# A two-layer decoder step on one core: the first layer's planned order is made anew

## The chip, the cores and the metric

The kernel runs on one core of one Trainium2 chip. The metric is the device time of one execution of the whole program, in microseconds (us); the median of several runs counts. In the names of the profile PE is the matrix engine (its matmuls; PEld its weight loads), DVE, ACT and POOL are the three engines for elementwise work, and SP is the engine that issues most transfers. A matmul's weights are its stationary operand.

## The reference

One step of a decoder with two layers, for a prompt of 512 tokens and 8 sequences of 8 new tokens (576 tokens in all, width 1024). The first layer is a gated DeltaNet, the second a differential attention over shared K and V with 64 pages of cache. Everything is float32. Only the first layer is touched by the change:

```python
shift, scale, gate = ada_split(c, ada_w_a, ada_b_a, 3)
h = modulate(x, norm_a, shift, scale)              # RMS norm, gain, shift
proj = h @ w_in                                    # q, k, v, z, beta, a
q, k, v = split(silu(causal_conv(conv_buf, qkv, conv_w)))   # width 4
a = tril(kb @ k.T * decay, -1)                     # per chunk of the tokens
t_inv = triangular_solve(eye + a, eye)             # an inverse per chunk and head
u, w = t_inv @ (v * beta), t_inv @ (kb * exp(g))
# along the chunks: v_new = u - w @ s;  o = (q * exp(g)) @ s + qk @ v_new
#                   s = s * exp(g_last) + (k * exp(g_last - g)).T @ v_new
y = (rms_norm(o, out_gain) * silu(z)) @ w_out
x = x + gate * y
```

The outputs are the tokens' results of both layers, the states of the DeltaNet and of the convolution (for the prompt and for each of the 8 sequences), and K and V.

## The kernel before

**Numbers.** Weights come in chunks of 128 x 1024. Each projection of a chunk is made in fp32r with a weight split in two parts, hi (the rounded weight, `whi`) and lo (the rest, `wlo`), and an activation split alike (`hhi`, `hlo`): 24 products of 128x288 for each half of the tokens (hlo with hi and hhi with hi for 8 slices, then hhi with lo for 8 slices). The other products are in plain fp32.

**First stretch.** `body` loads x, makes the norm, and goes in eight steps k over the eight slices of the features: a pair of products for shift and scale (`ada_pair`), then the slice's `modulate` (POOL and ACT). Three weights are loaded at k = WAT = 3, and their products are made slice by slice (`part`, recorded at L241). Then `phase_a` begins.

**The woven first layer.** The work on 16 heads, in 8 groups of two, is written as some dozens of generators: the conv of each tile (`conv`), the decays, `prep` (norms, k k and q k products, result `ckq`), the inverse of the chunks (`tinv_pe`, on 32x16 and 32x32 blocks), the `chain` over four chunks with its outputs, the samples' part (`tinv_s`, `sample_gdn`, `sample_states`), and `post` with its two heads. A generator yields the engine that it needs next, a cost in us and its conditions. `Weave.drive` steps that generator which the planner thinks can start first; of those that can start at once, that with the lowest rank. What is emitted so is pinned: on PE, ACT, DVE and POOL the order of the program is the order of the plan, and an engine waits at an instruction whose data isn't there. The plan's costs are numbers in the source; a transfer counts as landed a fixed time after its issue (7.0 for a weight).

**Weights in the woven part.** The weight sets j are in three rooms in turn (two of `whi`/`wlo`, one of two `wraw` tiles). `first_parts` issues hi (a transfer that casts, POOL's queue, L711), `negatives` writes its negative into lo on ACT (L719), `second_parts` adds the weight onto it by an accumulating transfer (POOL's queue, L727). `weave_proj` (L731) emits the products of a chunk in pieces of 4 products. The projections run in the order of `TILES`, then 8 chunks of the output projection (`out_half`) over the first eight heads. All woven products are recorded at L431, transposes at L435.

**Behind it.** `out_a` (the second half of the output projection) and the second layer are written out in order, with weights over `loadw`: a raw weight into `wraw` (SP's queue, L214), a cast on ACT (L217) and a difference on POOL (L218).

Of the kernel before, what the change touches and what calls it, by code (L numbers as in the profile page):

```python
# [26 lines left out]
G = 8  # L27
# [68 lines left out]
TILES = [(i + (t in "kq"), t) for i in range(G) for t in "vwkqzy" if i + (t in "kq") < G]  # L96
# [148 lines left out]
def ada_loads(K, W, A):  # L245
    at = 0.0
    for n, kt in enumerate(K.kts):
        yield None, 0, at, Room("araw")
        at = W.now + ADA
        ch = A.araw.tile([128, 8, 128], F32, name="araw")  # L250
        W.araw = ch, W.took[0]
        K.nc.sync.dma_start(out=ch[:], in_=K.ada[kt].rearrange("p (k m) -> p k m", m=128))
        W.done[("araw", n)] = W.now + 7.0, None
# [148 lines left out]
ENGINE = {"E": "E", "A": "A", "D": "D", "S": "D", "P": "P", "Q": "P"}  # L402


class Weave:
# [4 lines left out]

    def __init__(self, K):
        self.K, self.n, self.now = K, 0, 0.0
        self.free = dict.fromkeys("EADP", 0.0)
        self.port = 0.0
        self.done, self.live = {}, []
# [5 lines left out]
    def matmul(self, **kw):  # L421
# [6 lines left out]
        else:  # L428
            cost = 0.3 if n == 128 else 0.134 if n == 64 else 0.03 if n == 32 else 0.02
        self.cost += cost  # L430
        return self.K.nc.tensor.matmul(**kw)  # L431

    def transpose(self, **kw):
        self.cost += 0.11
        return self.K.nc.tensor.transpose(**kw)  # L435

# [3 lines left out]
    def leave(self, *rooms):  # L440

        self.later += [(self.left, r) for r in rooms]

# [18 lines left out]
    def ready(self, w):  # L462
# [3 lines left out]
        for c in [w[4]] + conds:  # L466
# [10 lines left out]
            x = max(x, t if e is None else t + ((0.0 if eng == "E" else 0.06) if eng and e and ENGINE[e] == ENGINE[eng] else PAD if eng == "E" else HOP))  # L477
        return x

    def drive(self):  # L480
        while self.live:
            x, w = math.inf, None
            for v in self.live:
# [8 lines left out]
            self.now, self.cost, self.later, self.rank, self.took = x, cost or 0.0, [], w[0], []  # L492
# [6 lines left out]
            w[4] = end  # L499
            if eng:  # L500
# [19 lines left out]
def gates(K, A, W, pss):  # L520
# [36 lines left out]
    W.done[("gcd",)] = W.now + 6.0, None  # L557
# [52 lines left out]
def phase_a(K, A, ctx, first):  # L610
# [14 lines left out]
    for name, bufs, roomy in (("u", UB, 1), ("y", YB, 1), ("v", 1, 1), ("z", 4, 1), ("ss", 1, 1), ("araw", 1, 1), ("cso", 2, 1),  # L625
                              ("kq", 2, 0), ("kt", 2, 0), ("vr", 4, 0), ("ck", 2, 0), ("adsb", 1, 0), ("ln", 1, 0),
# [7 lines left out]
    for name in ("pp", "pp", "pc", "po", "pa", "ps"):  # L634
        W.taken[name] += 1
    A.XC = A.ln.tile([128, 2, 8, 16], F32, name="XC")
# [7 lines left out]
    W.add(1, gates(K, A, W, first[0]))  # L644
    W.sets = {}
    W.add(4, first_parts(K, W, n + 1))
    W.add(4, negatives(K, W, n + 1))
    W.add(4, second_parts(K, W, n + 1))
# [3 lines left out]
    for s in groups:  # L652
        for rank, work in ((1, s.decays()), (1, s.prep()), (0, s.inverse()), (0, s.chunks()), (3, s.sample()), (2, s.post())):
# [10 lines left out]
HOP = 0.2  # L664
CONV = 6
PAD = 0.4
ADA = 11.5
UB = 2
YB = 1
# [31 lines left out]
def first_parts(K, W, n):  # L701


    for j, src in enumerate(sources(K, n)):
        yield "Q", 0.7, Room(f"set{j % 3}")
        if j % 3 < 2:
            hi, lo = (p.tile([128, 8, 128], F32R, name=n) for p, n in ((K.whi, "whi"), (K.wlo, "wlo")))
        else:
            hi, lo = (K.wraw.tile([128, 8, 128], F32, name="wraw")[:].bitcast(F32R) for _ in range(2))
        W.sets[j] = hi, lo, W.took[0]  # L710
        K.nc.gpsimd.dma_start(out=hi[:], in_=src)  # L711
        W.done[("hi", j)] = W.now + 7.0, None


def negatives(K, W, n):
    for j in range(n):
        yield "A", 1.05, ("hi", j)
        hi, lo, _ = W.sets[j]
        K.nc.scalar.activation(out=lo[:], in_=hi[:].bitcast(F32), func=AF.Copy, scale=-1.0)  # L719
# [3 lines left out]
def second_parts(K, W, n):  # L723

    for j, src in enumerate(sources(K, n)):
        yield "Q", 0.9, ("neg", j)
        K.nc.gpsimd.dma_start(out=W.sets[j][1][:], in_=src, accum_op=ALU.add)  # L727
        W.done[("w", j)] = W.now + 8.0, None


def weave_proj(K, W, j, evac, heads=None, slots=None):  # L731


    for half in range(2):
        yield "E", None, ("hi", j), Room("pp"), *([("h", heads), ("h", heads + 1)] if heads is not None else [])
        room, = W.took
# [1644 lines left out]
```

## Time and profile before

| | |
|---|---|
| runs | 1369.69, 1358.03, 1357.48 us, median 1358.03 |
| profiled execution | 1357.92 us, its span 1355.9 us |
| PE matmuls busy | 1252.6 us (92%), 13045 matmuls |
| DVE, ACT, POOL busy | 803.4, 719.5, 443.0 us |
| mean granted clock of PE | 0.955 of full speed |
| first stretch | 0 to about 62 us of the span |
| woven first layer | about 62 to 755 us |
| end of the first layer, second layer | from about 755 us |

PE busy is the time in which a matmul was under way, at whatever clock was granted. A clock of 0.50 means that the same work takes twice as long and still counts as busy. So both the idle time of PE and the stretches with a clock under 1.00 are to be looked at, and where they lie.

### The profile page before, as it was taken

How to read it: one execution, taken by the hardware profiler on the slowest of the kernel's cores; microseconds unless marked ns; L12 is line 12 of the kernel's file. 1: busy time of each engine (PE TensorE's matmuls, PEld its weight loads, DVE VectorE, ACT ScalarE, POOL GpSimd, SP SyncE). 2: the span in 40 equal slices, each digit the busy share in tenths (PEclk: the TensorE clock that was granted, in tenths of full speed). 3: DMA queues.
4: the chain of work that ended last, by engine and by line, in shares of the span. 5: the costliest groups of instructions: out<-in, count | busy, mean ns of one | idle time of the engine just before them, and what ended most of it. 6: DMA issues, size and time to landing. Idle time of an engine off the chain costs nothing. (4 is left out here: it accounts for less than half of the span.)

```text
span 1355.9 us, 33987 instructions
## 1 busy us (share of the span) xinstructions
PE 1252.6 (92%) x13045; PEld 1085.9 (80%) x13045; DVE 803.4 (59%) x2263; ACT 719.5 (53%) x1981; POOL 443.0 (33%) x812
## 2 busy tenths in 40 slices
PE   7889999999999898999889699699999999989988
PEld 4679898988878797897778598699888778757888
DVE  5467574766847575485652558688752455555461
ACT  3465767657675575765625332254443465555440
POOL 3423322222222122222111252945562343424232
PEclk7979999999999798999899799799999999999999
DMA  9186676584847466488475355121787877886333
GB/s 362 49 226 179 155 202 150 165 209 125 240 99 202 113 166 163 124 198 239 137 207 154 120 163 187 32 77 51 256 287 227 270 222 248 277 267 203 112 119 114
DMA packets 86643, 240.59 MB, mean 177 GB/s; under 512 B 14338, under 2 KB 26498, under 8 KB 86482
## 3 DMA queue, kind: packets, MB, share of 16 engines
q1 hardware_dynamic: 70642, 180.75, 40.5%
q0 software_dynamic: 15840, 57.68, 19.4%
q8 instruction: 103, 1.69, 0.5%
q14 instruction: 58, 0.48, 0.1%
HBM read 212.55 MB, written 25.84 MB: 176 GB/s over the span
## 5 line engine op out<-in xcount | busy, mean ns | idle before, releaser
L241 PE MATMUL pp<-hhi,whi 128*128 128x288 f32 x640 | 195.6, 309 | 18.8 <-ACT hhi L371 11.0
L241 PE MATMUL pp<-hlo,whi 128*128 128x288 f32 x640 | 194.1, 304 | 1.3 <-DVE hlo L1275 0.6
L241 PE MATMUL pp<-hhi,wlo 128*128 128x288 f32 x640 | 191.9, 301 | 0.0
L431 PE MATMUL pp<-hlo,whi 128*128 128x288 f32 x576 | 173.8, 322 | 2.0 <-DMA whi<-wall 1.7
L431 PE MATMUL pp<-hhi,whi 128*128 128x288 f32 x576 | 162.0, 301 | 0.0
L218 POOL TENSOR_TENSOR wlo<-wraw,whi 128x1024 fp32r<-128x1024 f32 x50 | 119.8, 2397 | 117.7 <-ACT whi L217 110.1
L241 PEld LDWEIGHTS pp<-hhi,whi 128*128 128x128 f32 x640 | 121.2, 191 | 28.0 <-ACT hhi L371 11.7
L241 PEld LDWEIGHTS pp<-hlo,whi 128*128 128x128 f32 x640 | 122.0, 191 | 7.5 <-issue 2.3
L431 PE MATMUL pp<-hhi,wraw 128*128 128x288 f32 x576 | 127.9, 307 | 0.0
L241 PEld LDWEIGHTS pp<-hhi,wlo 128*128 128x128 f32 x640 | 121.9, 191 | 2.1 <-issue 1.7
L431 PEld LDWEIGHTS pp<-hlo,whi 128*128 128x128 f32 x576 | 112.3, 195 | 8.1 <-issue 3.3
L431 PEld LDWEIGHTS pp<-hhi,whi 128*128 128x128 f32 x576 | 112.3, 195 | 0.2
L431 PE MATMUL pp<-hhi,wlo 128*128 128x288 f32 x576 | 102.5, 309 | 0.0
L217 ACT CAST whi<-wraw 128x1024 fp32r<-128x1024 f32 x50 | 52.3, 1048 | 89.7 <-PE pp L241 53.6
L431 PEld LDWEIGHTS pp<-hhi,wraw 128*128 128x128 f32 x576 | 97.8, 196 | 1.5 <-issue 0.8
L879 DVE SCALAR_TENSOR_TENSOR y<-u,vec,y 128x600 f32<-128x600 f32 x96 | 81.8, 853 | 18.2 <-ACT y L876 17.5
L431 PE MATMUL pp<-hlo,wraw 128*128 128x288 f32 x288 | 87.0, 321 | 0.0
L431 PEld LDWEIGHTS pp<-hhi,wlo 128*128 128x128 f32 x576 | 83.7, 193 | 2.6 <-issue 1.3
L727 POOL DMA_DIRECT2D wlo<-wall x37 | 32.9, 890 | 134.5 <-ACT wlo L719 66.9
L1535 POOL TENSOR_TENSOR wm<-w,con_mask 96x512 fp32r<-96x512 f32 x32 | 35.1, 1098 | 95.2 <-PE ps L431 90.5
L1940 DVE TENSOR_REDUCE mx<-sc 128x1 f32<-128x128 f32 (+3 forms) x64 | 31.4, 490 | 58.4 <-PE sc L1922 58.3
L1767 POOL COPY pg<-ptt 1x1 int32<-1x1 int32 x128 | 29.2, 237 | 100.7 <-PE pS L1797 40.3
(487 smaller groups left out, 3183.5 us busy)
## 6 DMA issues: line engine op xcount, KB each, us to landing
pg<-ck SPq DMA_DIRECT2D x64, 512.0 KB, 4.8
pg<-cv SPq DMA_DIRECT2D x64, 512.0 KB, 4.7
wraw<-wall SPq DMA_DIRECT2D x50, 512.0 KB, 4.1
araw<-ada SPq DMA_DIRECT2D x48, 512.0 KB, 4.7
whi<-wall POOLq DMA_DIRECT2D x37, 512.0 KB, 5.7
wlo<-wall POOLq DMA_DIRECT2D x37, 512.0 KB, 5.9
wraw<-wall POOLq DMA_DIRECT2D x36, 512.0 KB, 6.1
araw<-ada SPq DMA_DIRECT2D x8, 1024.0 KB, 13.8
```

The lines of the kernel that those rows point to most:

```text
L217: nc.scalar.copy(out=hi[:], in_=raw[:])
L218: nc.gpsimd.tensor_sub(out=lo[:], in0=raw[:], in1=hi[:].bitcast(F32))
L241: K.mm(out=ps[:, :HT], lhsT=w[a][:, k, :], rhs=h[b][:, k, half * HT:half * HT + HT], start=(k == 0 and a + b == 0), stop=(k == 7 and a == 1))
L431: return self.K.nc.tensor.matmul(**kw)
L727: K.nc.gpsimd.dma_start(out=W.sets[j][1][:], in_=src, accum_op=ALU.add)
L879: nc.vector.scalar_tensor_tensor(out=y[:, :YW], in0=u[:, j:j + YW], scalar=cw[j], in1=y[:, :YW], op0=ALU.mult, op1=ALU.add)
L1535: nc.gpsimd.tensor_mul(out=wm[:], in0=s.w3[:, hh, a, :].bitcast(F32).unsqueeze(1).to_broadcast([96, 4, 128]), in1=K.smaskb.unsqueeze(2).to ...
L1767: nc.gpsimd.tensor_copy(out=e, in_=P.ptt[0:1, i:i + 1])
L1940: nc.vector.tensor_reduce(out=mx[:, m:m + 1], in_=pss[m][:, :w], axis=AX.X, op=ALU.max, negate=True)
```

## The change

It touches the planner, the ranks of the generators, how finely some of them yield, a few buffers, and where the first weights are issued. What is computed stays the same, apart from zero products whose result nobody reads.

- Transfers are planned by a model of two queues (SP's and POOL's) that share the bandwidth, instead of fixed landings.
- The planner counts a cost (`TURN`) when PE goes between fp32r and fp32 work, and keeps a balance (`lean`) of the array's use. Sparse products (the inverse, the samples) yield "L" instead of "E" and are put behind all else while the balance is positive. In planned gaps of PE over 0.6 us it puts zero bf16 products of 128x224 (`fill`).
- `weave_proj` yields pieces of 8 products. The long runs of the inverse yield once more in between.
- Three conv input buffers (`u`) instead of two, two conv output buffers (`y`) instead of one; one tile of three slots for `ckq`, used by turns.
- The sets 0 and 1 are issued in the first stretch at k = 5, with their negatives and second parts at its end. The room made of `wraw` tiles is that of j % 3 = 1.
- The order of tiles in a group is v, k, w, q, z, y (it was v, w, k, q, z, y), and all ranks are new.

```diff
-TILES = [(i + (t in "kq"), t) for i in range(G) for t in "vwkqzy" if i + (t in "kq") < G]
+TILES = [(i + (t in "kq"), t) for i in range(G) for t in "vkwqzy" if i + (t in "kq") < G]
...
 class Weave:
     def matmul(self, **kw):
...
-        self.cost += cost
+        kind = 2 if rhs.dtype != F32 else 1 if m == k == 128 else 0
+        self.cost += cost + (TURN if kind != self.kind and (kind == 2 or kind + self.kind == 2) else 0.0)
+        self.kind = kind
+        self.use += n * (1 if kind == 2 else 2) * k * m * ARRAY
         return self.K.nc.tensor.matmul(**kw)
...
+    def fill(self, us):
+        n = int(us / FILLER)
+        zeros = self.K.cT[:, 0, 16:32].bitcast(BF16).unsqueeze(1).to_broadcast([128, 7, 32])
+        for _ in range(n):
+            self.K.nc.tensor.matmul(out=self.banks[0][:, HT:512].rearrange("p (a b) -> p a b", b=32),
+                                    lhsT=self.K.ident[:, 0:64].bitcast(BF16), rhs=zeros, start=True, stop=True)
+        self.lean = max(self.lean - (1 - FAIR) * n * FILLER, -CREDIT)
+        return n * FILLER
...
     def drive(self):
...
-                if y < x or y == x < math.inf and v[:2] < w[:2]:
-                    x, w = y, v
+                key = v[0] + (2000 if e == "L" and self.lean > LEAN else 0), v[1]
+                if y < x or y == x < math.inf and key < best:
+                    x, w, best = y, v, key
+            self.transfers(x)
...
+            pe, idle = eng in ("E", "L"), x - self.free["E"]
+            if pe and idle > GAP:
+                idle -= self.fill(idle - MARGIN)
...
+            if pe:
+                self.lean = max(self.lean + FAIR * (idle + self.cost) - self.use, -CREDIT)
...
-    W.add(4, first_parts(K, W, n + 1))
-    W.add(4, negatives(K, W, n + 1))
-    W.add(4, second_parts(K, W, n + 1))
+    W.add(-10, first_parts(K, W, n + 1))
+    W.add(-1, negatives(K, W, n + 1))
+    W.add(12, second_parts(K, W, n + 1))
...
-        for rank, work in ((1, s.decays()), (1, s.prep()), (0, s.inverse()), (0, s.chunks()), (3, s.sample()), (2, s.post())):
+        for rank, work in ((0, s.decays()), (4, s.prep()), (6, s.inverse()), (-10, s.chunks()), (5, s.sample()), (9, s.post())):
             W.add(10 * s.g + 10 + rank, work)
...
-UB = 2
-YB = 1
+UB = 3
+YB = 2
...
+def new_set(K, j, src):
+    if j % 3 == 1:
+        hi, lo = (K.wraw.tile([128, 8, 128], F32, name="wraw")[:].bitcast(F32R) for _ in range(2))
+    else:
+        hi, lo = (p.tile([128, 8, 128], F32R, name=n) for p, n in ((K.whi, "whi"), (K.wlo, "wlo")))
+    K.nc.gpsimd.dma_start(out=hi[:], in_=src)
+    return hi, lo
...
 def weave_proj(K, W, j, evac, heads=None, slots=None):
...
-            steps = [(0, (k, k + 1)) for k in range(0, 8, 2)] + [(1, range(4)), (1, range(4, 8))]
+            steps = [(0, range(k, k + 4)) for k in range(0, 8, 4)] + [(1, range(8))]
...
 def tinv_pe(K, A, W, ck, WF):
...
-    yield "E", None
     for n in range(8):
+        if n % 4 == 0:
+            yield "L", None
         for p, at in blocks:
             W.matmul(out=pz[p, 1, n, :], lhsT=WC[p, n, :], rhs=V[p, n, 0:16], start=True, stop=True, tile_position=at)
...
 def body(tc, ins, outs, dump=None):
...
+                    if k == 5:
+                        K.early = [new_set(K, j, src) for j, src in enumerate(sources(K, 2))]
+                for (hi, lo), src in zip(K.early, sources(K, 2)):
+                    negative(K, hi, lo)
+                    second_part(K, lo, src)
```

How this moves the instructions is seen in three places. `XC`, `WC` and `V` are blocks of the inverse, `ob`, `osb` and `Ss` belong to the samples and outputs, `pp` is a bank of a projection.

On PE, in the inverse of one group in the middle of the woven part, the order before is this (behind the last row here the two kinds of x4 rows go on by turns, 16 rows in all, 64 products):

```order
L431 MATMUL pp<-hhi,wraw 128x288 x5
L431 MATMUL pa<-XC,ckq 32x16 x32
L431 MATMUL pt<-P_5117,L_5103 64x64 x2
L431 MATMUL ps<-Ss,kTm 32x256 x8
L431 MATMUL pa<-V_135,WC 32x16 x4
L431 MATMUL pa<-WC,V_135 32x16 x4
```

Of the change, at the same place of a group, from the end of the first 32 sparse products over the first 32 of the 64:

```order
L437 MATMUL pa<-XC,ckq 32x16 x32
L443 MATMUL ps<-con_ident,ob 128x128 x4
L437 MATMUL pp<-hlo,whi 128x288
L437 MATMUL pp<-hhi,whi 128x288
...
L437 MATMUL pa<-V_133,WC 32x16 x4
L437 MATMUL pa<-WC,V_133 32x16 x4
...
L443 MATMUL ps<-con_ident,osb 128x64
L437 MATMUL pp<-hhi,wlo 128x288 x8
```

Where 32 and 64 sparse products stood with ten small ones between them, now 8 products of a projection and a row of transposes stand between the first 32 and the next, and 8 more products before the third 32.

On POOL, at the end of the first stretch, the order before has the first weights of the woven part behind everything:

```order
L372 TENSOR_TENSOR hlo<-scr,hhi 128x64
L592 MEMSET z 128x576
L593 MEMSET z 128x4
L594 MEMSET z 128x8
L526 MEMSET Ss 128x640
L820 MEMSET u 128x3
L821 COPY u<-cso 128x8x3
L820 MEMSET u 128x3
L821 COPY u<-cso 128x8x3
L711 DMA whi<-wall 128x1024 x2
```

Of the change, with L780 the transfer of hi, L790 that of lo, and L368 to L372 the steps of `modulate`:

```order
L780 DMA whi<-wall 128x1024
L368 TENSOR_TENSOR scr<-x,rstd 128x64
L218 TENSOR_TENSOR wlo<-wraw,whi 128x1024
L369 TENSOR_TENSOR scr<-scr,g1a 128x64
L370 TENSOR_TENSOR scr<-scr,mod 128x64
L368 TENSOR_TENSOR scr<-x,rstd 128x64
L790 DMA wlo<-wall 128x1024
L369 TENSOR_TENSOR scr<-scr,g1a 128x64
L790 DMA wraw<-wall 128x1024
L372 TENSOR_TENSOR hlo<-scr,hhi 128x64
```

The weights of the sets 0 and 1 are now issued among the steps of `modulate`, at rows 25 and 36 of POOL's program; the first stood at row 58.

On SP, at the end of the woven part (`o_sts` are the samples' new states, `x1d` the first layer's sums, `wraw<-wall` at L214 the raw weights of the part behind it), before:

```order
L1614 DMA x1d<-y 128x576
L1578 DMA scr<-ogd_89 128x576
L214 DMA wraw<-wall 128x1024 x2
L1614 DMA x1d<-y 128x576
L214 DMA wraw<-wall 128x1024
L1550 DMA o_sts<-Ss 128x1024 x2
L1657 DMA xin<-x1d 128x288 x5
```

and of the change:

```order
L1647 DMA o_sts<-Ss 128x1024
L1713 DMA x1d<-y 128x576
L214 DMA wraw<-wall 128x1024
L1194 DMA o_stp<-S 128x256
L214 DMA wraw<-wall 128x1024
L1713 DMA x1d<-y 128x576
L1676 DMA scr<-ogd_89 128x576
L1713 DMA x1d<-y 128x576
L1757 DMA xin<-x1d 128x288 x3
```

The samples' last states are written ahead of the raw weights instead of behind them, and two raw weights stand ahead of the last two `x1d` (before, ahead of the last one).

More of the change, by code (lines that the diff above doesn't have):

```diff
@@ L252, in ada_loads @@
         K.nc.sync.dma_start(out=ch[:], in_=K.ada[kt].rearrange("p (k m) -> p k m", m=128))
-        W.done[("araw", n)] = W.now + 7.0, None
+        W.load("S", 1.6, "araw", n)
 def ada_units(K, W, A):
@@ L442, in leave, with load, transfers @@
         self.later += [(self.left, r) for r in rooms]
+    def load(self, queue, us, *name):
+        self.coming.append((self.now + LATENCY, self.n, queue, us, name))
+        self.coming.sort()
+        self.n += 1
+    def transfers(self, until):
+        while True:
+            act = [q for q in self.queues.values() if q]
+            rate = SHARED if len(act) > 1 else 1.0
+            lands = self.clock + min(q[0][0] for q in act) / rate if act else math.inf
+            comes = self.coming[0][0] if self.coming else math.inf
+            t = max(self.clock, min(lands, comes))
+            if t > until or t == math.inf:
+                return
+            for q in act:
+                q[0][0] -= (t - self.clock) * rate
+            self.clock = t
+            if comes <= lands:
+                _, _, q, us, name = self.coming.pop(0)
+                self.queues[q].append([us, name])
+            else:
+                for q in act:
+                    if q[0][0] < 1e-9:
+                        self.done[q.pop(0)[1]] = t + LATE, None
+                return
     def set(self, *name):
@@ L556, in gates @@
     W.leave(("z", 0))
-    W.done[("gcd",)] = W.now + 6.0, None
+    W.load("S", 0.3, "gcd")
     yield "S", 2.0, Room("z")
@@ L635, in phase_a @@
         W.taken[name] += 1
+    A.ckq = A.rows.tile([128, 3, 8, 128], F32, name="ckq")
     A.XC = A.ln.tile([128, 2, 8, 16], F32, name="XC")
@@ L644, in phase_a @@
     W.add(1, gates(K, A, W, first[0]))
+    W.banks = first[0]
     W.sets = {}
-    W.add(4, first_parts(K, W, n + 1))
-    W.add(4, negatives(K, W, n + 1))
-    W.add(4, second_parts(K, W, n + 1))
+    for j in range(len(K.early)):
+        W.done[("w", j)] = 2.0 + j, None
+    W.add(-10, first_parts(K, W, n + 1))
+    W.add(-1, negatives(K, W, n + 1))
+    W.add(12, second_parts(K, W, n + 1))
     for i in range(2):
@@ L664 @@
 HOP = 0.2
+LATENCY = 2.3
+SHARED = 0.56
+LATE = 0.6
+TURN = 0.085
+ARRAY = 1 / 2400 / 16384
+FAIR = 0.55
+LEAN = 0
+CREDIT = 0.2
+FILLER = 0.105
+GAP = 0.6
+MARGIN = 0.2
 CONV = 6
@@ L826, in evac @@
         us = u[:, 3 + SEQ:].rearrange("p (b e) -> p b e", e=11)
[L827 removed]
+        yield "A", 0.47 if half else 0.4
         if half == 0:
@@ L1276, in head @@
         W.set("og", g, hh)
-        yield None, 0, W.now + 4.0
+        yield None, 0, *(() if last else (("ogd", h),))
         W.leave(zt)
```

178 lines of the change are left out of this document (98 added, 80 removed).

## The prediction

> **What bounds the kernel now.** I read the page's first two parts, then the table by stage, then the waits of PE, and only then single rows.
>
> ```profile
> span 1355.9 us, 33987 instructions
> PE 1252.6 (92%) x13045; PEld 1085.9 (80%) x13045; DVE 803.4 (59%) x2263; ACT 719.5 (53%) x1981; POOL 443.0 (33%) x812
> PEclk7979999999999798999899799799999999999999
> ```
>
> PE is busy for 92% of the span and everything else for 59% or less, so PE is the bound. The clock row shows seven slices at 7 or 8 tenths, all among the first 26 of 40. The table by stage (length; PE busy; then the others; then granted clock, share of the transfer engines, GB/s) gives the woven first layer in three pieces:
>
> ```profile
> 60.00:100.00 40.00, 30.21 (x245) 26.48 (x246) 23.24 (x58) 27.32 (x68) 12.88 (x35) 0.79 0.82 216
> 100.00:740.00 640.00, 604.40 (x7043) 538.22 (x7034) 398.74 (x1210) 399.41 (x1195) 152.41 (x297) 0.96 0.64 171
> 740.00:790.00 50.00, 37.23 (x214) 32.90 (x213) 24.48 (x61) 20.09 (x46) 15.08 (x11) 0.80 0.41 122
> ```
>
> PE idles 9.8 us at the start, 35.6 in the middle and 12.8 at the end. The clock costs busy time times what is missing to 1.00: 6.3, 24.2 and 7.4 us. Together this is 96 us. An order of the same products can win no more than that, so 1358 - 96 = 1262 is a floor. In the middle one wait is the largest by far:
>
> ```profile
> PE pa L431 <- issue: 15.8, 8, 4.0
> 375.58 0.21 PE L431 MATMUL pa<-WC,V 32*32 32x16 f32 x3 [2.35 <-issue]
> 458.94 0.23 PE L431 MATMUL pa<-WC,V 32*32 32x16 f32 x2 [3.70 <-issue]
> 531.38 0.24 PE L431 MATMUL pa<-WC,V 32*32 32x16 f32 x3 [3.99 <-issue]
> 627.69 0.17 PE L431 MATMUL pa<-WC,V 32*32 32x16 f32 x1 [1.72 <-issue]
> 710.85 0.26 PE L431 MATMUL pa<-XC,ckq 32*32 32x32 f32 x1 [3.02 <-issue]
> ```
>
> Eight waits, 15.8 us, behind which no engine and no transfer stands, all in the sparse products of the inverse. Are they instructions that have not yet come? The counts of PE and PEld records from the start up to three of them say so:
>
> ```profile
> 0.00:374.50 374.50, 347.49 (x3770) 301.43 (x3770) 239.75 (x683) 231.00 (x654) 110.12 (x234) 0.95 0.67 187
> 0.00:457.00 457.00, 424.29 (x4658) 367.83 (x4659) 292.02 (x853) 285.94 (x825) 129.73 (x274) 0.95 0.65 181
> 0.00:530.00 530.00, 492.11 (x5419) 429.26 (x5420) 336.73 (x983) 329.60 (x951) 147.24 (x309) 0.94 0.64 177
> q8 instruction: 103, 1.69, 0.5%
> ```
>
> The sums are 7540, 9317 and 10839, their differences 1777 = 7 x 256 - 15 and 1522 = 6 x 256 - 14. The stalls sit a whole number of 256 instructions apart (short of it by some two a block, which the records don't count), and the instruction queue moved 103 pieces of 1.69 MB / 103 = 16.4 KB. So I take it that PE runs dry at the edge of a block, where the block was used up faster than the next one came. Each stall is followed by a slow clock:
>
> ```profile
> 372.00:384.00 12.00, 9.65 (x258) 7.37 (x254) 5.12 (x26) 6.59 (x17) 1.30 (x3) 0.86 0.43 87
> 456.00:476.00 20.00, 17.05 (x137) 15.01 (x136) 7.62 (x26) 9.22 (x24) 3.27 (x7) 0.66 0.39 93
> 528.00:544.00 16.00, 12.62 (x202) 10.68 (x205) 4.91 (x18) 7.29 (x18) 3.54 (x8) 0.79 0.59 155
> 624.00:636.00 12.00, 9.89 (x236) 7.53 (x225) 6.24 (x23) 4.73 (x13) 2.09 (x3) 0.86 0.68 139
> 708.00:720.00 12.00, 9.15 (x107) 8.62 (x108) 1.33 (x4) 5.48 (x13) 2.38 (x4) 0.86 0.89 267
> ```
>
> Length times missing clock is 1.7 + 6.8 + 3.4 + 1.7 + 1.7 = 15.3 us. A stall thus costs about twice its length.
>
> The Trainium skill, page "Runtime: NRT & Kernel Launch", section "Instruction fetch mechanics", says that instructions come in 16 KiB blocks of 256 and that the cost of crossing a block is "mostly hidden". The size agrees with the 16.4 KB here; "hidden" doesn't agree with the 15.8 us. By that rule these waits would have another cause and splitting the sparse runs would bring nothing: that is the first rival below.
>
> **The change part by part.** The sum goes against the profiled execution, 1357.92 us (span 1355.9 and 2.0 around it), which is the median 1358.03 within 0.1.
>
> *Stalls (sparse runs split, "L" put behind dense work).* A sparse product takes little:
>
> ```profile
> L431 PE MATMUL pa<-WC,V 32*32 32x16 f32 (+1 forms) x768 | 16.5, 185 | 11.9 <-issue 11.8
> 85.14 0.38 PE L431 MATMUL pp<-hlo,whi 128*128 128x288 f32 x1
> 85.36 0.30 PE L431 MATMUL pp<-hhi,whi 128*128 128x288 f32 x1
> 85.50 0.30 PE L431 MATMUL pp<-hlo,whi 128*128 128x288 f32 x1
> ```
>
> 16.5 us for 768 is 0.021 us each; a dense product follows the one before it after 0.14. A block of 256 instructions holds 128 products: 2.7 us if all are sparse, 18 if all are dense. I went over both orders with these spacings, for every 256 instructions in a row: the least work in any such stretch is 1.25 us before and 2.2 us after, and the number of blocks' lengths that hold under 3 us falls from 7.0 to 1.9. If a block's coming takes a time T and the stall is T less the work in the block, T = 4.3 us gives the 15.75 us of before, and the same T gives about 6 after. So the term is -10 for the stalls and, by the ratio 15.3 to 15.8, -10 for the clock: **-20**. Bounds: 0 (T isn't the reason) and -31 (all go).
>
> *Start (early weights, third u buffer).*
>
> ```profile
> 40.00:60.00 20.00, 20.00 (x157) 15.71 (x157) 8.98 (x24) 6.44 (x16) 8.44 (x16) 1.00 0.04 12
> 61.91 0.29 PE L241 MATMUL ps<-hhi,wlo 128*128 128x288 f32 x1
> 66.41 1.08 PE L431 MATMUL pa<-araw,cT 128*32 128x128 f32 x16 [4.20 <-DMA araw<-ada]
> 69.14 0.61 PE L431 MATMUL pp<-hlo,whi 128*128 128x288 f32 x1 [1.66 <-DMA whi<-wall]
> ```
>
> Between 40 and 60 us the transfers are nearly idle (0.04), then PE waits 4.2 us for an ada weight and 1.7 for the first woven weight, and the clock falls. Two weights issued in the idle stretch take the second wait away, and the queue in front of the first gets shorter. What is late next are the conv buffers and the banks of the first three tiles, for PE evacuates those before it may go on; the order shows 30 zero products before the first projection and 41 more early on, so the plan itself still sees gaps there. I take half of the 9.8 idle and 6.3 clock, rounded down: **-7**, bounds 0 and -14. The two early transfers stand in POOL's queue amid `modulate`; a wait of POOL at row 36 (for a free `whi`) or 42 (for the negative on ACT) would hold up the slices of the first stretch, where PE is at 20.00 of 20. POOL is at 8.44 of 20 there, so I cost it at nothing; uncovered it would be up to 4 us, within the bound.
>
> *The gap between two groups and the throttled stretch.*
>
> ```profile
> 640.00:656.00 16.00, 11.20 (x78) 9.54 (x79) 10.18 (x20) 12.62 (x32) 3.17 (x3) 0.57 0.89 261
> 432.00:444.00 12.00, 11.04 (x63) 9.31 (x63) 7.93 (x25) 6.70 (x21) 3.67 (x7) 0.72 0.94 292
> ```
>
> The first loses 4.8 us idle and 16 x 0.43 = 6.9 of clock. The new order has 52 zero products near there, so the idle stays about as it is and only the clock is kept: **-5**, bounds 0 and -10. What is left of the middle, 35.6 - 15.8 - 4.8 = 15 us idle and 24.2 - 15.3 - 6.9 = 2 of clock (the second row, 3.4, says it is a little more), is short waits for ACT, DVE and transfers. Two y buffers, three u buffers, three `ckq` slots and the queue model aim at those: **-9**, bounds +5 (the new order has waits of its own) and -15.
>
> *Changes of kind.* After a transpose the next dense product is followed at 0.22 instead of 0.14 (85.14 to 85.36, then 85.50): 0.08 each. The order counts 559 changes to or from fp32r before and 507 after: 52 x 0.08 = **-4**, bounds 0 and -5.
>
> *Zero products.* 182 in all. No row shows one; by size 224 / 288 x 0.14 = 0.11 us each, 20 us if all lay beside nothing, 0 if all lie in gaps. They are put only where the plan sees a gap, so I take a tenth: **+2**, bounds 0 and +20.
>
> *End.*
>
> ```profile
> 744.00:779.00 35.00, 23.78 (x135) 20.43 (x134) 19.53 (x53) 12.99 (x31) 7.94 (x7) 0.80 0.39 120
> 756.29 0.37 PE L241 MATMUL pp<-hhi,whi 128*128 128x288 f32 x1 [2.41 <-DVE y L1564]
> 775.39 3.01 DMA o_sts<-Ss
> 778.50 1.99 ACT L217 CAST whi<-wraw 128x1024 fp32r<-128x1024 f32 x2 [8.84 <-DMA o_sts<-Ss]
> 779.60 0.61 PE L241 MATMUL pb<-hhi,whi 128*128 128x288 f32 x1 [5.40 <-ACT whi L217]
> 779.62 4.70 POOL wlo L218 x2
> ```
>
> The path there runs over the samples' last states: their write (3.01) is done at 778.4, then ACT casts a raw weight, and PE, idle for 5.4 us, starts on it; the differences on POOL follow (4.70). In these 35 us stands PE work of 23.78 at clock 0.80, 19.0 at full speed. The new order has the states done 250 rows before the last projection and raw weights loaded ahead of two `x1d`, since set 53 no longer holds `wraw`. The states go from the path; next is the last chunk's own evacuation and `x1d` (the 2.41 at 756.29 is of this kind), and 58 zero products (6 us) stand ahead of the last projection, so the plan sees a gap there still. Of 16 us I take half: **-8**, bounds 0 and -16.
>
> Sum: -20 - 7 - 5 - 9 - 4 + 2 - 8 = -51. The plan's costs are the planner's and the chip's differ; an engine that is pinned to a wrong order waits where none waited. I take off 6 for this, by choice, two fifths of the 15 us that such short waits cost now: **-45**, so 1313 us.
>
> **The rivals.**
>
> *1. The stalls stay.* For it: the rule cited, and that each group still has 32 or 64 sparse products in a few microseconds, at a repeat of 320 rows a group. Against it: the multiples of 256. Then -20 is gone: -25, **1333 us**.
>
> *2. Nearly all the loss goes.* If the zero products keep the clock everywhere and stalls vanish: -31 - 14 - 10 - 12 - 4 + 2 - 10 = -79, with the same 6 taken off -73: **1285 us**. Against it: DVE and ACT with 399 us of 640 have bursts that PE meets.
>
> *3. Slower: a group's own recurrence becomes the bound.* Sparse steps are put behind dense pieces, which are now 8 products (8 x 0.14 = 1.1 us) instead of 4, and the chain of a group goes through them one after the other.
>
> ```profile
> 650.03 0.80 PE L431 MATMUL pc<-vr,WF 128*128 128x128 f32 x2 [2.61 <-ACT WF L1393]
> 699.73 0.27 PE L435 MATMUL ps<-con_ident,osb 64*128 64x64 f32 x1
> ```
>
> From the first product of a chain to the group's last head are 49.7 us; the inverse ahead of it is entered every (710.85 - 375.58) / 4 = 83.8 us. There is room of some 34 us for the inverse and its preparation. If the some 30 steps of a group's inverse, samples and chain each wait one more piece (0.55 to 1.1 us), 16 to 33 us are added: from 34 on the group is the bound, and each us beyond shows seven times. At 37 it is +21 and the gains of the start and end remain: 1358 + 21 - 7 = **1372 us**. Against it: the order repeats after 320 PE rows with no zero product between the groups 1 to 6, so the plan sees PE full there.
>
> *4. Gain and loss cancel.* The new waits take what the old ones gave, or the zero products displace work at their full 20 us: **1352 us**.
>
> **How the numbers follow.** Forecast 0.52 (1296 to 1328 by its own bounds), rival 1 0.17, rival 2 0.13, rival 3 0.08, rival 4 0.10. 1% (13.6 us) is about what a measurement of this kernel can tell from no change. Faster by more: forecast and rivals 1 and 2, 0.82; within 1%: rival 4, 0.10; slower: rival 3, 0.08. The range takes in the forecast and rivals 1 and 2 down to their middle and up to near rival 4: 1283 to 1347, with about 0.2 left out.
>
> **What would show it.** Right: the waits of sparse products "<-issue" fall from 15.8 us to 6 or less and the slices with 7 tenths of clock in the middle vanish; the first woven product comes about 3 us after the first stretch; the stretch from the last group's chain to `out_a` is 8 us shorter; the zero products' busy time lies where PE would be idle. Wrong: if the issue waits are as long as before at other instructions, rival 1; if PE waits for ACT or DVE at the inverse and the groups come more than 84 us apart, rival 3; if the granted clock is above 0.98 and PE idles under 20 us in the first layer, rival 2. What I can least tell is how closely the new plan matches the chip.

## The result and the profile after

The changed kernel takes 1314.93 us in the median (1313.22 to 1317.32), the kernel before on the same chip 1358.79: a ratio of 0.9654, 95% interval 0.9608 to 0.9701. The profiled execution has a span of 1313.1 us, 42.8 less than before. 1313 was forecast. The parts of the sum came out much less well than the sum, and that is the subject of this section and the next ones. A profile shows one execution of each kernel.

The page of the kernel after:

```profile
span 1313.1 us, 34330 instructions
PE 1245.7 (95%) x13227; PEld 1083.6 (83%) x13227; DVE 807.7 (62%) x2263; ACT 715.5 (54%) x1981; POOL 444.0 (34%) x811
PEclk8999999999999999999999998999999999989999
```

The slices at 7 tenths are gone from the first layer. PE is busy for about as many microseconds as before, at a higher clock and with 182 zero products more. I cut both executions at the same products: first woven product, first product of `out_a`, its norm, first and last product of the second layer's cache scores. Before (length; PE busy; ...; clock, share of the transfer engines, GB/s):

```profile
69.14:756.29 687.15, 644.99 (x7345) 575.22 (x7345) 427.04 (x1292) 430.30 (x1279) 164.18 (x321) 0.95 0.64 172
756.29:816.54 60.25, 48.90 (x302) 44.86 (x303) 30.55 (x54) 18.34 (x30) 23.87 (x12) 0.83 0.50 152
946.25:1176.70 230.45, 226.16 (x2654) 184.15 (x2656) 122.12 (x329) 113.31 (x290) 101.52 (x215) 1.00 0.77 251
1176.70:1355.90 179.20, 164.91 (x1625) 137.77 (x1616) 86.57 (x250) 77.70 (x206) 55.25 (x81) 0.99 0.53 170
```

and after:

```profile
64.26:722.98 658.72, 643.11 (x7527) 574.03 (x7525) 439.01 (x1316) 430.81 (x1285) 165.33 (x321) 1.00 0.68 179
722.98:766.17 43.19, 39.52 (x288) 38.47 (x289) 23.74 (x33) 14.64 (x23) 22.08 (x9) 1.00 0.52 155
895.96:1129.00 233.04, 227.83 (x2657) 185.03 (x2656) 122.17 (x330) 113.47 (x290) 102.25 (x215) 0.99 0.75 248
1129.00:1313.10 184.10, 169.42 (x1625) 141.16 (x1613) 86.77 (x250) 77.61 (x206) 55.23 (x81) 0.96 0.53 166
```

The first woven product comes 4.9 us earlier, the woven stretch is 28.4 shorter, `out_a` 17.1 shorter; the piece between (129.7 and 129.8) is the same; and the second layer, which the change doesn't touch, is 2.6 and 4.9 longer. -4.9 - 28.4 - 17.1 + 7.6 = -42.8.

In the woven stretch PE's idle time fell from 42.2 to 15.6 us, and the clock, at half speed for 64.6 us of it before, isn't lowered once. Dense products take 378.5 instead of 396.9 us from each one's start to the next, waits left out; the 151 zero products of this stretch take 14.8. So idle -26.6, dense -18.4, zero products +14.8, the rest +1.7. PE's waits in the middle and single rows:

```profile
PE pp L450 <- DVE y L1656: 2.9, 1, 2.9
PE pc L437 <- ACT wk L1223: 2.8, 5, 0.6
PE ps L437 <- issue: 1.3, 4, 0.4
61.36 3.13 PE L450 MATMUL pp<-cT,con_ident 128*128 128x224 bf16 x31 [0.22 <-ACT v L587]
64.26 0.38 PE L437 MATMUL pp<-hlo,whi 128*128 128x288 f32 x1
281.69 1.07 PE L437 MATMUL ps<-Ss,kTm 128*32 128x256 f32 x16 [0.30 <-issue]
356.22 1.07 PE L437 MATMUL ps<-Ss,kTm 128*32 128x256 f32 x16 [0.30 <-issue]
430.75 1.07 PE L437 MATMUL ps<-Ss,kTm 128*32 128x256 f32 x16 [0.30 <-issue]
505.36 1.07 PE L437 MATMUL ps<-Ss,kTm 128*32 128x256 f32 x16 [0.35 <-issue]
708.35 5.72 PE L450 MATMUL pp<-cT,con_ident 128*128 128x224 bf16 x58 [2.91 <-DVE y L1656]
```

The 15.8 us of issue waits at the inverse are gone; four of 0.3 are left, at another product. The same row comes back after 74.53, 74.53 and 74.61 us. Over these three groups PE is busy for 220.5 of 223.7 us, so in the middle of the layer a group now takes little more than PE's work for it, and not the some 83 us of before.

What made the second layer longer is mainly a clock that fell behind waits for cache pages (after; and the same piece before, 1212 to 1224, where such waits left the clock at 1.00):

```profile
1164.00:1176.00 12.00, 9.09 (x109) 6.95 (x109) 4.67 (x13) 3.76 (x9) 1.27 (x5) 0.78 0.85 293
1176.00:1188.00 12.00, 12.00 (x116) 8.48 (x116) 5.18 (x13) 6.04 (x16) 4.61 (x10) 0.79 0.49 153
1166.83 0.62 PE L1940 MATMUL po<-pg,pTs 128*8 128x128 f32 x16 [1.11 <-DMA pg<-cv]
1169.45 0.62 PE L1940 MATMUL po<-pg,pTs 128*8 128x128 f32 x16 [1.41 <-DMA pg<-cv]
1212.00:1224.00 12.00, 9.38 (x145) 6.59 (x145) 6.26 (x16) 5.76 (x14) 2.40 (x8) 1.00 0.83 291
```

That the change is what made it longer isn't shown. From the second layer's norm to the end the fourteen profiles of this study take 539.3 to 548.0 us; the kernel before is the shortest of all of them, and a kernel with the old planner (the run with the room of `wraw` moved) has 547.7.

### The profile page after: what moved, and what is told of

Its sections match the earlier page's. It is cut to its first block, busy times and chain, and to the rows that moved or that the text cites. A ratio compares the mean times of both kernels' runs of the same rounds, so it can differ in the third digit from the quotient of the medians.

```text
span 1313.1 us, 34330 instructions
## 1 busy us (share of the span) xinstructions
PE 1245.7 (95%) x13227; PEld 1083.6 (83%) x13227; DVE 807.7 (62%) x2263; ACT 715.5 (54%) x1981; POOL 444.0 (34%) x811
## 4 chain that ended last, share of the span: by engine, by line
PE 79%; DVE 6%; DMA 6%; POOL 3%; issue 3%; ACT 2%; SPq 1%; POOLq 0%; DVEq 0%; ACTq 0%
PE pp L437 27%; PE pp L241 14%; PE pa L437 6%; PE pc L437 6%; PE ps L437 2%; PE po L1940 2%; PE pt L437 2%; PE pS L1897 2%; DMA pg<-cv 2%; PE pt L443 2%; PE sc L241 2%; PE pv L2060 1%; DMA pg<-ck 1%; PE sc L2020 1%; DMA araw<-ada 1%
## 5 line engine op out<-in xcount | busy, mean ns | idle before, releaser
L241 PE MATMUL pp<-hhi,whi 128*128 128x288 f32 x640 | 195.0, 308 | 18.8 <-ACT hhi L371 11.9
L241 PE MATMUL pp<-hlo,whi 128*128 128x288 f32 x640 | 193.5, 303 | 2.7 <-DVE hlo L1681 1.9
L241 PE MATMUL pp<-hhi,wlo 128*128 128x288 f32 x640 | 191.7, 301 | 0.2 <-POOL wlo L218 0.2
L437 PE MATMUL pp<-hlo,whi 128*128 128x288 f32 x576 | 166.2, 310 | 0.1
L437 PE MATMUL pp<-hhi,whi 128*128 128x288 f32 x576 | 156.9, 294 | 0.0
L241 PEld LDWEIGHTS pp<-hhi,whi 128*128 128x128 f32 x640 | 121.0, 190 | 27.1 <-ACT hhi L371 12.6
L241 PEld LDWEIGHTS pp<-hlo,whi 128*128 128x128 f32 x640 | 121.7, 190 | 8.1 <-DVE hlo L1681 2.4
L437 PE MATMUL pp<-hhi,wraw 128*128 128x288 f32 x576 | 124.2, 300 | 0.0
L437 PEld LDWEIGHTS pp<-hlo,whi 128*128 128x128 f32 x576 | 108.6, 189 | 6.2 <-issue 3.4
L437 PEld LDWEIGHTS pp<-hhi,whi 128*128 128x128 f32 x576 | 108.4, 188 | 0.4
L437 PEld LDWEIGHTS pp<-hhi,wraw 128*128 128x128 f32 x576 | 93.3, 188 | 5.3 <-issue 4.9
L437 PE MATMUL pp<-hhi,wlo 128*128 128x288 f32 x576 | 96.8, 302 | 0.0
L970 DVE SCALAR_TENSOR_TENSOR y<-u,vec,y 128x600 f32<-128x600 f32 x96 | 84.9, 884 | 11.4 <-ACT y L967 9.9
L437 PE MATMUL pp<-hlo,wraw 128*128 128x288 f32 x288 | 83.1, 312 | 0.1
L790 POOL DMA_DIRECT2D wlo<-wall x37 | 32.9, 889 | 124.2 <-ACT wlo L785 94.3
L437 PEld LDWEIGHTS pp<-hlo,wraw 128*128 128x128 f32 x288 | 54.1, 188 | 2.4 <-issue 0.7
```

Source lines behind the costliest of these rows:

```text
L241: K.mm(out=ps[:, :HT], lhsT=w[a][:, k, :], rhs=h[b][:, k, half * HT:half * HT + HT], start=(k == 0 and a + b == 0), stop=(k == 7 and a == 1))
L790: K.nc.gpsimd.dma_start(out=lo[:], in_=src, accum_op=ALU.add)
L970: nc.vector.scalar_tensor_tensor(out=y[:, :YW], in0=u[:, j:j + YW], scalar=cw[j], in1=y[:, :YW], op0=ALU.mult, op1=ALU.add)
```

## The experiments

Each time stands as the ratio to the kernel before on the same chip, with its interval; the change itself is at 0.9654 (0.9608 to 0.9701), and 0.01 is 13.6 us. Except where an order is said to be kept, the planner makes a new one, so a kernel differs from its neighbour by more than its edit says.

**Are the issue waits edges of instruction blocks?** 128 more PE instructions ahead of everything, in the kernel before:

```diff
+                for _ in range(32):
+                    nc.tensor.matmul(out=warm[:, 0:16], lhsT=A.WFs[0][:, 0, :], rhs=A.WFs[0][:, 0, 0:16], start=True, stop=True)
```

> The kernel before with 32 small fp32 products (128x16, result unread) behind its six warm-up products, in time in which PE waits for x: 128 more PE instructions, half of a block of 256, ahead of everything. Theory A (stalls at the edges of blocks of instructions): the stalls '<-issue' come at other products than before, 128 instructions away from the old places, still a whole number of 256 apart; some fall into dense work and vanish, others appear; their sum changes by several us from 15.8 and the time by up to 10 us either way. Rival (the stalls belong to the products themselves, for instance a bank, a clock or the queue of the samples' part): the same products (pa<-WC,V in the same groups, 375 to 711 us) stall for the same 15.8 us within 2, and the time is 1358 within 4.

Ratio 1.002 (0.9977 to 1.0064). The added products weren't free: the first woven product comes at 74.4 us instead of 69.1, and the woven stretch is 4.5 us shorter. The waits moved to other products, with about the same sum (14.5 us), which I had expected to change by more:

```profile
PE pa L431 <- issue: 14.1, 7, 3.7
220.15 0.58 PE L431 MATMUL pa<-XC,ckq 32*32 32x32 f32 x14 [3.69 <-issue]
532.09 0.63 PE L431 MATMUL pa<-araw,cT 128*32 128x128 f32 x11 [2.71 <-issue]
627.85 0.17 PE L431 MATMUL pa<-WC,V 32*32 32x16 f32 x1 [2.80 <-issue]
```

The largest, 3.69 us at 220, stands where the kernel before had none, and the 3.70 of before at 459 is gone. Counting every PE instruction of the program up to the waiting one shows where they stand: before, the waits stand at 256 n - 62 with n = 24, 30, 37, 43, 51, 52 and 58; here at n = 10, 16, 30, 31, 38, 44, 52 and 58, so at other instructions and the same edges. In the fourteen profiles of this study there are 67 waits "<-issue" of over 0.25 us between 62 and 760 us; 56 stand at such an edge, and the 11 others are all at one product of the samples' states (`ps<-Ss,kTm`, 0.3 us each) or of the gates (`pt<-con_ident,Ss`, 2.5). The instruction queue's transfers are in the trace too: before, each waiting product starts 2.3 to 2.45 us after the start of a 16.4 KB transfer. From the edge before to the edge that waits, the seven took 6.42, 4.91, 5.74, 6.91, 4.27, 5.57 and 6.33 us. This isn't a least time for a block. The kernel before has one with the inverse's sparse products that was used up in 2.00 us, from the edge at n = 8 to the one at n = 9, and no wait follows:

```profile
141.78:143.78 2.00, 2.00 (x136) 1.97 (x136) 0.88 (x5) 1.89 (x5) 0.33 (x2) 1.00 0.97 129
```

There the last transfer had started at 140.43, ahead of both edges; at the seven waits it started only behind the edge before. So theory A holds for the place of the waits, and a single time T for a block doesn't.

**Zero products left out**, all else in its order:

```diff
-        for _ in range(n):
+        for _ in range(0):
```

> The changed kernel with its 182 zero products left out; every other instruction keeps its order (the planner still counts the gaps as filled). Theory A (the clock falls because PE stalls after sparse runs; the zero products only bridge the few planned gaps): the middle, 100 to 600 us, keeps its clock of 1.00 and its groups 74.5 us apart; the clock falls for some us behind the gaps at 632 and 708 us and at the start, at most 3 x 4 us at half clock, so 6 us lost, while up to 4 us of displaced work come back: 1313 to 1321 us against 1315. Theory B (the zero products are what holds the clock in the whole layer): the granted clock in 100 to 600 us falls to 0.97 or less and the time rises by 15 us or more.

Ratio 0.9681 (0.9611 to 0.9750); 1312.66 us. This is theory A. The clock falls only where the gaps were:

```profile
60.00:100.00 40.00, 36.48 (x322) 32.75 (x321) 27.30 (x66) 31.31 (x84) 13.98 (x41) 0.96 0.74 191
100.00:600.00 500.00, 494.33 (x6014) 439.67 (x6014) 348.93 (x1054) 344.40 (x1042) 133.00 (x264) 1.00 0.68 177
600.00:720.00 120.00, 110.23 (x1067) 96.69 (x1065) 65.66 (x198) 59.71 (x173) 23.71 (x30) 0.94 0.66 190
```

The first woven product comes at 61.3 us instead of 64.3: the gap that the plan had seen at the start wasn't there, and 31 zero products filled PE's own time. They cost about what they keep.

**Whole sparse runs**, not split and not put behind dense work:

```diff
-LEAN = 0
+LEAN = 1e9
...
         if n % 4 == 0:
-            yield "L", None
```

> The changed kernel with the sparse products of the inverse no longer split and no longer put behind dense work (LEAN so high that the balance never decides). The plan around it is made anew, with 244 zero products. Theory A: stalls of the kind '<-issue' come back, 8 us or more in the first layer (least work in 256 instructions is again 1.25 us), each with some us of half clock behind it; granted clock of 100 to 600 us about 0.97; 1330 to 1340 us. Theory B (the stalls of before had another cause, and the gain is that of the new ranks, buffers and queue model): the stalls stay under 2 us and the time within 5 us of 1315.

Ratio 0.9622 (0.9568 to 0.9675): not slower, though waits at four edges (5.5 us) and 13.7 us of half clock are back between 100 us and `out_a`:

```profile
PE pa L437 <- issue: 4.3, 3, 1.8
PE ps L437 <- issue: 1.2, 1, 1.2
```

By its time theory A fell here; theory B wanted under 2 us of stalls, and there are 5.5. The same without zero products:

> The changed kernel with whole sparse runs (not split, not put behind) and without zero products; the order is that of the run with the bursts, less its 244 zero products. Theory A (zero products cost a little more than the clock that they keep): some 5 us less than that run's 1308, so 1300 to 1306 us, a granted clock of 100 to 600 us of 0.98 or more. Rival (with bursts and without zero products the clock falls as it did before): granted clock of that stretch 0.97 or less, 1312 us or more.

Ratio 0.9595 (0.9545 to 0.9644), the lowest ratio of all (1308.55 us), but its interval meets that of the change.

```profile
PE pa L437 <- issue: 10.0, 8, 3.1
100.00:600.00 500.00, 483.48 (x5961) 435.60 (x5961) 338.63 (x1048) 338.57 (x1037) 132.31 (x263) 0.98 0.66 175
```

The result lies between the two theories. The waits at edges are nearly all back (11.9 us with 1.9 at dense products), with 37.5 us of half clock ahead of `out_a`, and yet the time is no longer. So the waits do stand at edges, but under the new ranks taking them out by splitting is worth nothing measurable. Against the run without zero products this one has 12.4 us more idle in the woven stretch and 7.7 us less PE time in the same products: 630.0 instead of 637.7, at a lower clock. Its order changes to or from fp32r 464 times, the split one 504. Sparse pieces between dense ones cost PE time; that the 40 changes are the whole reason wasn't tried by itself. The traces show what such a change takes at full clock, in medians of the kernel before: the dense product ahead of 64x64 ones is followed after 0.22 us instead of 0.13, the last 64x64 one after 0.15 instead of 0.06, and the next dense one after 0.24 instead of 0.13.

**Ranks.** All ranks as before, with the rest of the change:

```diff
-        for rank, work in ((0, s.decays()), (4, s.prep()), (6, s.inverse()), (-10, s.chunks()), (5, s.sample()), (9, s.post())):
+        for rank, work in ((1, s.decays()), (1, s.prep()), (0, s.inverse()), (0, s.chunks()), (3, s.sample()), (2, s.post())):
...
-            W.add(10 * g + 17, self.chain(hh))
+            W.add(10 * g + 10, self.chain(hh))
```

> The changed kernel with every rank of a generator as it was before (weights, groups, conv, chain, samples, post); all else of the change stays, and the plan is made anew. The plan now has 428 zero products instead of 182, that is 246 x 0.1 = 25 us more of planned gaps on PE. Theory A (the new ranks are what keeps PE fed; the stalls at block edges are only a part): 1335 to 1345 us, with 400 zero products' busy time on PE. Rival (the ranks matter little beside the stalls, the buffers and the early weights): within 6 us of 1315.

Ratio 1.0116 (1.0083 to 1.0149): 1.2% slower than the kernel before, where both theories expected it to be faster.

```profile
PE pc L437 <- ACT wv L1242: 7.3, 17, 1.0
L450 PE MATMUL pp<-cT,con_ident 128*128 128x224 bf16 x428 | 51.9, 274 | 5.5 <-DVE z L944 4.2 <-DVE y L1656 1.1 <-ACT v L587 0.2
```

428 zero products fill PE for 51.9 us and the groups come up to 96 us apart. I read this as the third rival, in another kernel: sparse work put behind everything, with these ranks, makes the group's own chain the bound. Old ranks and whole sparse runs:

> The changed kernel with the old ranks, and with whole sparse runs that are not put behind dense work; the queue model, the buffers, the early weights, the counted changes of kind and the pieces of 8 products stay. 230 zero products (428 with the old ranks and the demotion, 182 in the change). Theory A (the new ranks only make good what the demotion of sparse work costs; the gain is that of buffers and early weights): 1310 to 1322 us. Rival (the new ranks are worth tens of us by themselves): 1335 us or more, and groups 80 us apart again.

Ratio 0.9818 (0.9770 to 0.9866). So under the old ranks splitting and demoting cost 0.0298, some 40 us; under the new ones the same step (0.9622 to 0.9654) costs nothing that the intervals show.

```profile
PE pa L437 <- issue: 19.8, 6, 4.2
```

Against the run with whole runs and new ranks this is 0.0196 more, 27 us, and 1335.16 us is just at the rival's bound, though the groups come 77 us apart on average and not 80: the ranks are the largest single part found. Of it 14 us are waits at edges (19.8 against 5.5), and those are partly luck: by the prediction's way of counting, an estimate, the two orders give some 16 and 13 us over all alignments.

**Buffers.** Two `u` (`UB = 2`), then also one `y` (`YB = 1`):

> The changed kernel with two conv input buffers (u) as before, instead of three; plan made anew, 278 zero products, 96 x 0.1 = 10 us more of planned gaps. Theory A (the third buffer lets projections run on while a conv is late): 1322 to 1330 us. Rival (the conv is not what PE waits for): within 4 us of 1315.

Ratio 0.9692 (0.9649 to 0.9735).

> The changed kernel with the conv buffers of before: two for inputs and one for outputs (a condition is added in out_half so that the second half waits for the first). Plan made anew, 289 zero products. Theory A (the third input buffer is worth 6 us, the second output buffer little more): 1318 to 1328 us. Rival (one output buffer is what held the conv, and so the groups, in the kernel before): 1335 us or more, with groups 80 us apart.

Ratio 0.9739 (0.9691 to 0.9787). The two buffers are worth some 12 us, as theory A had it, at intervals that just overlap; the third input buffer by itself 5, which the intervals don't separate from nothing.

**Queue model** (`load` sets fixed landings):

```diff
+        self.done[name] = self.now + fix[name[0]], None
```

> The changed kernel with the fixed landings of before in the planner (7.0 us for a weight, 8.0 for its second part and so on) instead of the model of two queues; plan made anew, 202 zero products. Theory A (the queue model changes the plan little): within 5 us of 1315. Rival (real landings later than planned make PE wait): PE waits for whi, wlo or wraw from transfers for 5 us or more in the first layer, 1322 to 1332 us.

Ratio 0.9635 (0.9586 to 0.9683): no difference.

**Early weights.** Left out of the change (`K.early = []`):

> The changed kernel without the two early weight sets: all weights of the woven part are issued behind the first stretch, as before. Theory A (my term: half of 14 us of loss at the start): the first woven product comes 4 to 5 us later than the 64.3 us of the change, the clock falls once at the start, and the time is 1320 to 1324 us. Rival (the start is hidden behind the evacuation of the first tiles and zero products keep the clock): the same within 3 us, 1312 to 1318 us.

Ratio 0.9762 (0.9702 to 0.9822), 15 us more than the change, but not by the theory: the first woven product comes at 65.3 us, only 1.0 later, and the clock holds to 100 us. The loss is in the new order behind it, with 6.6 us at three edges and 20.5 us of half clock. In the kernel before, first the room of `wraw` moved alone (`j % 3 != 1` for `j % 3 < 2`), then with the early weights:

> The kernel before with one edit: the room of two wraw tiles is that of the sets j % 3 = 1 instead of 2, so that the last woven projection holds no wraw and the raw weights of the part behind can be loaded earlier. Theory A (my term for the end): the stretch from the first product of out_a to its norm (60.2 us before, 43.2 after the change) shrinks by 8 us or more, and the time is 1344 to 1351 us. Rival (that stretch waits for the samples' last states and their write, which stay where they are): 1358 within 4.

Ratio 1.0030 (0.9994 to 1.0067). This is the rival: `out_a` takes 58.3 us to its norm, and its waits stand.

```profile
PE pp L241 <- DVE y L1564: 6.5, 1, 6.5
PE pb L241 <- ACT whi L217: 5.0, 1, 5.0
```

> The kernel before with the set of wraw tiles moved as in the run with that edit alone, and with the sets 0 and 1 issued at k = 5 of the first stretch, negatives and second parts at its end; ranks, buffers and planner as before. Theory A (the start is worth 5 to 12 us by itself): 5 to 12 us less than the run with the set moved. Rival (without the third conv buffer and the new plan PE waits for other things at the start): the same within 3 us of that run.

Ratio 0.9986 (0.9951 to 1.0020).

```profile
61.37 0.30 PE L431 MATMUL pp<-hlo,whi 128*128 128x288 f32 x1
74.81 0.45 PE L435 MATMUL pt<-con_ident,Ss 128*128 128x128 f32 x1 [4.97 <-ACT Ss L569]
```

The times don't decide: this is 0.0044, 6 us, less than the run with the room moved, as theory A had it, but at intervals that overlap. The traces speak for the rival. The first woven product comes 7.8 us earlier than before, and 13 us later PE waits 5.0 us for ACT in the gates. The inverse of the first group is entered at 136.5 us instead of 138.2: most of the gain is gone before it. `out_a` begins at 761.2 us, and at 762.2 in the run with the room moved; both reach its norm at 820.4 to 820.5.

## Why the prediction was right, point by point

- **Stalls, -20.** The waits went, 15.5 us at edges to none, further than the 6 that I had left; the place was right to the instruction. The step that failed is the price. That a stall "costs about twice its length" was taken as time to be won, and I charged nothing for the means: the run with 11.9 us of such waits is as fast as the one without. T isn't one number either: 4.3 to 6.9 us at the waits, and a block used up in 2.00 us without one. The 0.021 us for a sparse product was misread: two groups of such products overlap, and the 32x16 ones follow each other after 0.009, so 128 of them take some 1.2 us and not 2.7. And whether an order stalls depends on where the edges happen to fall: orders that the same count puts at about the same (some 13 us) had 5.5 and 11.9.
- **Start, -7.** -4.9 at the first woven product, of which 3 us of zero products had to be waited out. But the reason was wrong: by itself the edit gives 7.8 us there and nothing by the layer's norm. It is hidden, which I had named only for what comes "late next".
- **Gaps and short waits, -5 and -9.** Right in kind: the clock doesn't fall, and idle that isn't at edges went from 27 to 16 us. By the runs without them this is the buffers (some 12 us for both) and the ranks; the queue model did nothing measurable.
- **Changes of kind, -4.** Not seen. 941 fp32 products of full height take 114.4 us, 933 took 110.9: 0.12 each both times, in spite of the higher clock. The step that failed is that only half of the change was read. The row ahead of the three that I showed is this one:

```profile
84.79 0.60 PE L435 MATMUL pt<-con_ident,k 128*128 128x128 f32 x4
```

Four transposes take 0.35 us to the dense product at 85.14, 0.10 less than at the 0.112 us at which transposes follow each other elsewhere: the last one is followed after 0.03. That gives back the 0.08 which the dense product behind takes more. Changes of this kind, between dense products and those in fp32 that use the whole array, fell from 299 in the kernel before to 220 in the run without zero products; those to or from products on a part of the array, most of which cost time, rose from 358 to 438, and with whole sparse runs there are 328.

- **Zero products, +2.** All 182 take 17.7 us of PE, counted from each one's start to the next; in the profiles they cost 5.8 us up to `out_a`, and without them the clock falls for 17 us; the runs can't tell the two kernels apart.
- **End, -8.** -17.1, more than my bound of 16 on all. The reason was wrong: the raw weights are not it. What the new order has and the moved room alone doesn't is that the samples' last states are done long before. That this is the reason was not tried alone. Every kernel with the new planner has this stretch at 41.6 to 46.7 us, that with old ranks too, where the last state's write lands 9.1 us behind the first product of `out_a` (before, 22.1 behind it; after, 30.4 ahead of it). So the cause of this gain stays open.
- **Slips in the sums.** Half of 9.8 + 6.3 is 8, not 7. Rival 3 names the gains of start and end and takes off the start's 7 alone. The 1352 of rival 4 and the forecast's 1296 to 1328 aren't added up from terms. The 83.8 us between groups were taken from rows of two different steps; the same row of the inverse (370.1 and 702.0 us) gives 83.0. None of these decides the outcome.
- **The second layer** was costed at nothing. Its 7.6 us lie within what the fourteen profiles differ by there (539.3 to 548.0), so they may be chance.

So the sum is right and its terms are not. The start and the woven stretch were forecast at -43 and gave -33.3; the end at -8 and gave -17.1; the second layer at nothing and gave +7.6; and 6 had been taken off by choice. That these meet within 2 us of the forecast is luck.

By the prediction's own signs the picture is in part that of its second rival, whose time was 1285. Of the forecast's signs three came (the issue waits, the clock slices, the first woven product 3 us behind the first stretch). One didn't: from the first product of the last group's chain to `out_a` it is 42.7 us instead of 33.6, and not 8 shorter. The rival's own sign came in full: from 60 us to the norm behind `out_a` the granted clock is 1.00 and PE idles 19.5 us, where the rival asked for over 0.98 and under 20. What was costed too low is the means. In that stretch idle time fell by 39.9 us. Of the 88.7 us at half clock PE was busy in 68.4; with a dense product at 0.240 us there and 0.133 at full clock, I estimate that these held 30.5 us too many. Of these 70 us the layer gave 50.4, and the zero products that helped to keep the clock took 17.7 of the rest.

## What to carry to other kernels

A wait can be explained to the instruction and still not be worth its length: before a stall is priced, ask what the order without it makes PE do instead, and test the price by putting the stall back into the new kernel. Where a planner sets the order, no edit can be undone by itself; a part that gives 7.8 us at one place of the old order gave nothing at its end, and the same part left out of the new order cost 15. Ranks and yields belong together: demoting the sparse work under the old ranks made the kernel slower than it had been. And when a forecast comes true, go through the signs that were set for each rival as well: here the number was the forecast's, and the clock and idle time were a rival's.

## What the runs showed of the hardware

- PE's instructions come in blocks of 256, one transfer of 16.4 KB each (103 for 26424 instructions, which are 103.2 blocks). At the 56 waits the first product of a block starts 2.2 to 3.1 us after the start of a transfer, and that transfer had started behind the edge before. In the kernel before a block of mostly dense work takes 14.7 us (from n = 18 to 19) and the shortest one, at the inverse, 2.00.
- The half clock comes in pieces of 3.4 us. A wait of 1.72 us was followed by one such piece, one of 3.70 by four, one of 3.99 by two, and one of 2.71 (at 532 us in the shifted kernel) by none. In it a dense product follows the one before after 0.240 us, at full clock after 0.133: not quite twice.
